# Loading the positions and the bias table from GpSimd's queue instead of SP's, in a two-layer encoder trunk

## The chip, the core and the metric

The kernel runs on one core of a Trainium2 chip. A core has engines that each work through their own queue of instructions: TensorE (PE) multiplies matrices, VectorE (DVE) and ScalarE (ACT) do elementwise work and reductions, GpSimd (POOL) does a little of that and issues DMAs, and SyncE (SP) issues most of the DMAs. ScalarE issues a few as well. Engines wait for each other and for DMAs through semaphores; within an engine's queue, an instruction that waits holds up everything behind it.

The metric is the device time of one execution in microseconds (us); the time of a kernel is the median of its runs.

## What is computed

A trunk of two layers over 256 tokens of width 2048, in float32. Each layer is an attention sub-layer (12 mixer heads and 4 heads into 256 memory tokens, one combined input projection, one output projection) and a squared-ReLU MLP of width 8192. All mixer heads of both layers add a relative-position bias, which is looked up in a small table by the distance of two positions:

```python
def t5_bucket(rel):
    half = N_BUCKETS // 2
    max_exact = half // 2
    side = jnp.where(rel > 0, half, 0)
    n = jnp.abs(rel)
    n_f = jnp.maximum(n, 1).astype(jnp.float32)
    large = max_exact + (jnp.log(n_f / max_exact) / math.log(MAX_DISTANCE / max_exact)
                         * (half - max_exact)).astype(jnp.int32)
    large = jnp.minimum(large, half - 1)
    return side + jnp.where(n < max_exact, n, large)

def rel_bias_lookup(rel_bias, rel):
    return jnp.take(rel_bias, t5_bucket(rel), axis=0)
...
for i in range(DEPTH):
    h = rms_norm(x, norm_attn[i])
    ...
    proj = h @ w_in_a[j]                  # layer 0; w_in_b in layer 1
    ...
    x = x + heads @ w_out[i]
    h = rms_norm(x, norm_mlp[i])
    x = x + jnp.square(jax.nn.relu(h @ w_up[i])) @ w_down[i]
```

The change touches the inputs of that lookup: the 256 integer positions, and `rel_bias`, the table of 32 buckets by 12 heads.

## The kernel before

**Tiling.** Every float32 product is made of three passes: an operand is split into `hi`, its value rounded to a shorter float, and `lo`, what is left; the passes are hi by hi, hi by lo and lo by hi. For a weight, ScalarE casts the loaded `raw` to `hi` (L355) and VectorE subtracts to get `lo` (L356). For the activations of the first chunk, ScalarE makes the `hi` half of `x` with the norm's gain (L351) and VectorE its `lo` half (L352).

**The first chunk.** Layer 0's input projection goes in chunks of 512 output columns (`chunk_tok`, L414). A chunk has 8 pieces of 512 KB, a piece has two blocks of 128 rows of k, and a block is 6 matmuls (L426 to L428): two groups of tokens by three passes. That makes 16 blocks and 96 matmuls a chunk. In the first chunk only (`lead=first`), each piece is loaded in two halves, one for each block, and before each block `first` loads parts of the input `xs` from ScalarE's queue (L994) and makes that block's `x`. From the second chunk on, whole pieces are fetched ahead (`fetch`, L303). `raw`, `hi` and `lo` have four buffers each, so SP's next weight load waits until VectorE has made the `lo` of the piece four before.

**Tasks.** Small work is cut into stages and put between pieces. `tick` (L163), called after each piece, runs the next stage of the first task that is due. `prep` (L1014) is the task that prepares the bias; it becomes due 5 ticks after the start. Its stages are:

- `bias_distance` (L705): two loads by SP, the positions along the free dimension on all 128 partitions (`pq`, a `t1k` buffer, L707) and the positions by partition (`pk`, an `sm` buffer, L709); two subtractions on GpSimd (L712); a cast to float on VectorE (L714).
- `bias_size` (L716) and three times `bias_steps` (L722): the bucket number by compares and adds on VectorE (L718, L719, L724).
- `bias_side` (L726): the sign's half on VectorE (L728, L730), and a store of the bucket numbers to DRAM as `bkt` (L731).
- `bias_table` (L733): `tab` is cleared on VectorE (L735), four copies of the table are loaded by SP (L737), and it is split in three parts of short floats (L741, L743).

After that, eight tasks (`bias_hot`, `bias_rows`) load `bkt` back from GpSimd's queue (L756) spread over the partitions, compare it with the bucket numbers on VectorE (L758), and use TensorE to look up the bias (L767).

**Order.** The text of the kernel gives priorities, not the final order in each engine's queue: when the program is built, an instruction may be set earlier than its place in the text if it is expected to be ready. The trace shows this: the clearing of `tab` (L735) and GpSimd's L747, both from the last stage of `prep`, run in the first 2 us. In the queue of one engine the built order is fixed.

Of the kernel before, what the change touches and what calls it, by code (L numbers as in the profile page):

```python
# [17 lines left out]
I32 = mybir.dt.int32  # L18
# [4 lines left out]
P = 128  # L23
S = 256
# [32 lines left out]
def trunk(ctx: ExitStack, tc: tile.TileContext, xin, xtok, memin, pos, rel, gcol, rows,  # L57
          w_a, w_b, w_mem, w_out, w_up, w_down, out):
    nc = tc.nc
# [10 lines left out]
    def nm(s):  # L70
        uid[0] += 1
        return f"{s}{uid[0]}"
# [25 lines left out]
    def big(shape):  # L98
        return xp.tile(shape, F32, tag="big", name=nm("big"), bufs=1)

    def t2k(shape, dt=F32):
        return tp.tile(shape, dt, tag="t2k", name=nm("t2k"), bufs=6)

    def t1k():
        return tp.tile([P, 256], F32, tag="t1k", name=nm("t1k"), bufs=4)

    def small(n):
        return tp.tile([P, n], F32, tag="sm", name=nm("sm"), bufs=36)
# [593 lines left out]
    bsv = dp.tile([P, 12 * 2 * S], F32, name="bsv")  # L702
    tabs = {}

    def bias_distance():  # L705
        pq = t1k().bitcast(I32)
        nc.sync.dma_start(pq, pos.rearrange("(a s) -> a s", a=1).broadcast_to([P, S]))  # L707
        pk = small(2).bitcast(I32)
        nc.sync.dma_start(pk, pos.rearrange("(t p) -> p t", p=P))  # L709
        dl = t2k([P, 2, S], I32)  # L710
        for t in range(2):
            nc.gpsimd.tensor_tensor(dl[:, t, :], pk[:, t:t + 1].broadcast_to([P, S]), pq, op=ALU.subtract)  # L712
        tabs["f"] = t2k([P, 2, S])
        nc.vector.tensor_copy(tabs["f"], dl)  # L714
# [7 lines left out]
    def bias_steps(*at):  # L722
        for thr in at:
            nc.vector.scalar_tensor_tensor(tabs["b"], tabs["n"], float(thr), tabs["b"], op0=ALU.is_ge, op1=ALU.add)  # L724
# [8 lines left out]
    def bias_table():  # L733
        tab = cp.tile([P, 48], F32, name="tab")
        nc.vector.memset(tab, 0.0)  # L735
        for g in range(4):
            nc.sync.dma_start(tab[32 * g:32 * g + 32, 12 * g:12 * g + 12], rel)  # L737
        parts = []
        for i in range(3):
            part = cp.tile([P, 48], BF16, name=f"tab{i}")  # L740
            nc.vector.tensor_copy(part, tab)  # L741
            if i < 2:
                nc.vector.tensor_tensor(tab, tab, part, op=ALU.subtract)  # L743
            parts.append(part)
        it = cp.tile([P, 1], I32, name="iti")
        for g in range(4):
            nc.gpsimd.iota(it[32 * g:32 * g + 32, :], pattern=[[0, 1]], base=0, channel_multiplier=1)  # L747
        itf = cp.tile([P, 1], F32, name="itf")
        nc.vector.tensor_copy(itf, it)
        tabs["parts"], tabs["iota"] = parts, itf  # L750
# [251 lines left out]
    def first(k):  # L1002
# [5 lines left out]
        elif k % 2 == 0:  # L1008
# [2 lines left out]

    bias = big([P, 12, 2, S])
    Task([scalars], wait=4)
    prep = Task([bias_distance, bias_size, lambda: bias_steps(12, 16), lambda: bias_steps(23, 32), lambda: bias_steps(46, 64, 91),  # L1014
                 bias_side, bias_table], wait=5, gap=1)
    rows_done = [Task([lambda i=i: bias_hot(i), lambda i=i: bias_rows(i, bias)], [prep], wait=BW) for i in range(8)]
# [112 lines left out]
```

## Time and profile before

| | us |
|---|---|
| median of 3 runs | 2106.43 |
| the runs | 2107.10, 2103.86, 2106.43 |
| the profiled execution | 2105.52 |
| its span, first to last instruction | 2103.7 |

The profile is taken from one execution. Its views name a line and an engine, the tile written and the tiles read (`out<-in`), the shape and the count; a bracket at the end of a row says how long the engine stood idle before it and what it waited for. `SPq`, `ACTq` and `POOLq` rows are DMA issues or waits of that engine's queue; the transfer itself goes on after the issue. Starts are in us from the first instruction. Matmul rows last longer than the step from one matmul to the next, because matmuls are pipelined.

Before the change, SP's queue has the first eight weight loads (0.75 to 7.78 us), then a load of parameter rows, one of the four table loads (8.38), and then weight loads with the positions, parts of the residual input (L1000) and the other three table loads in between, up to 24.55 us.

### The profile page before, as it was taken

To read this page: it belongs to the slowest core of one execution; us is meant where nothing else is said; L and a number is where in the kernel's file an instruction comes from. 1 tells how busy PE (TensorE), PEld (TensorE's weight loads), DVE (VectorE), ACT (ScalarE), POOL (GpSimd) and SP (SyncE) were. 2 spreads that over 40 slices of the span, in tenths; PEclk is the share of its full clock that TensorE was granted. 3 is DMA by queue.
4 is the path that set the end of the run, shared out by engine and by line. 5 is a ranking of instruction groups with operands and counts; after the bars stand their busy time and mean duration, and the time that the engine had idled before them with its cause. 6 is when DMAs were issued, how large, how long until landed. Compare 5 with 4: busy or idle time off the path is not lost.

```text
span 2103.7 us, 30034 instructions
## 1 busy us (share of the span) xinstructions
PE 2094.0 (100%) x10924; PEld 1773.7 (84%) x10924; DVE 1641.4 (78%) x2463; ACT 1175.7 (56%) x1782; POOL 115.8 (6%) x211
## 2 busy tenths in 40 slices
PE   9999999999999999999999999999999999999999
PEld 7878878888888888888888888888888888888887
DVE  7667788866666679999996678886676667999998
ACT  6466585554444456656655556554444445666664
POOL 1200020000011000000000000000001100000000
PEclk9999999999999999999999999999999999999999
DMA  8865554677788778878866656457788977888884
GB/s 293 239 209 154 164 183 159 186 236 238 255 298 304 257 244 277 299 242 274 304 241 205 180 164 184 159 178 250 256 267 300 310 230 279 272 285 288 287 292 145
DMA packets 150452, 504.18 MB, mean 240 GB/s; under 512 B 17952, under 2 KB 18720, under 8 KB 150048
## 3 DMA queue, kind: packets, MB, share of 16 engines
q1 hardware_dynamic: 129696, 433.53, 63.0%
q0 software_dynamic: 19168, 66.60, 9.9%
q10 hardware_dynamic: 1440, 2.15, 0.3%
q8 instruction: 85, 1.39, 0.3%
q14 instruction: 63, 0.52, 0.1%
HBM read 464.85 MB, written 37.36 MB: 239 GB/s over the span
## 4 chain that ended last, share of the span: by engine, by line
PE 97%; DMA 1%; DVE 1%; ACT 1%; issue 0%; SPq 0%; POOL 0%; POOLq 0%
PE mm L439 11%; PE aux L439 11%; PE mm L466 7%; PE mm L467 7%; PE aux L467 7%; PE aux L466 7%; PE mm L465 7%; PE aux L465 7%; PE mm L426 6%; PE mm L427 6%; PE mm L428 6%; PE mm L443 6%; PE aux L443 6%; DMA raw<-in_w_a 1%; PE aux L567 1%; PE aux L538 1%
## 5 line engine op out<-in xcount | busy, mean ns | idle before, releaser
L356 DVE TENSOR_TENSOR lo<-raw,hi 128x1024 fp32r<-128x1024 f32 (+1 forms) x616 | 739.7, 1212 | 364.6 <-ACT hi L355 361.4
L355 ACT CAST hi<-raw 128x1024 fp32r<-128x1024 f32 (+1 forms) x616 | 632.2, 1040 | 576.6 <-PE mm L439 158.9
L426 PE MATMUL mm<-hi,x 128*128 128x512 f32 x640 | 256.7, 403 | 0.6 <-ACT hi L355 0.6
L427 PE MATMUL mm<-lo,x 128*128 128x512 f32 x640 | 251.9, 394 | 2.2 <-DVE lo L356 2.0
L428 PE MATMUL mm<-hi,x 128*128 128x512 f32 x640 | 251.7, 393 | 0.0
L439 PE MATMUL mm<-x,hi 128*128 128x512 f32 x1024 | 246.9, 391 | 0.0
L439 PE MATMUL aux<-x,hi 128*128 128x512 f32 x1024 | 246.9, 391 | 0.0
L439 PEld LDWEIGHTS mm<-x,hi 128*128 128x128 f32 x1024 | 188.2, 188 | 36.4
L439 PEld LDWEIGHTS aux<-x,hi 128*128 128x128 f32 x1024 | 188.2, 188 | 36.4
L355 ACT CAST x<-big 128x1024 fp32r<-128x1024 f32 x106 | 110.6, 1053 | 142.0 <-DVE big L291 114.8
L465 PE MATMUL mm<-hi,h 128*128 128x512 f32 x446 | 174.0, 390 | 0.0
L466 PE MATMUL mm<-lo,h 128*128 128x512 f32 x446 | 173.6, 389 | 0.0
L467 PE MATMUL mm<-hi,h 128*128 128x512 f32 x446 | 173.5, 389 | 0.0
L465 PE MATMUL aux<-hi,h 128*128 128x512 f32 x444 | 172.9, 390 | 0.0
L467 PE MATMUL aux<-hi,h 128*128 128x512 f32 x444 | 172.6, 389 | 0.0
L466 PE MATMUL aux<-lo,h 128*128 128x512 f32 x444 | 172.6, 389 | 0.0
L427 PEld LDWEIGHTS mm<-lo,x 128*128 128x128 f32 x640 | 121.0, 189 | 25.4 <-DVE lo L356 3.8
L428 PEld LDWEIGHTS mm<-hi,x 128*128 128x128 f32 x640 | 120.6, 188 | 25.5
L426 PEld LDWEIGHTS mm<-hi,x 128*128 128x128 f32 x640 | 120.8, 189 | 24.6 <-ACT hi L355 1.0
L443 PEld LDWEIGHTS aux<-x,lo 128*128 128x128 f32 x1024 | 131.3, 191 | 5.0
L443 PEld LDWEIGHTS mm<-x,lo 128*128 128x128 f32 x1024 | 131.1, 191 | 4.8
L443 PE MATMUL mm<-x,lo 128*128 128x256 f32 x1024 | 133.0, 283 | 0.0
(269 smaller groups left out, 3120.2 us busy)
## 6 DMA issues: line engine op xcount, KB each, us to landing
raw<-in_w_up SPq DMA_DIRECT2D x256, 512.0 KB, 4.6
raw<-in_w_down SPq DMA_DIRECT2D x140, 512.0 KB, 4.6
big<-in_w_down SPq DMA_DIRECT2D x97, 512.0 KB, 5.0
raw<-in_w_a SPq DMA_DIRECT2D x72, 512.0 KB, 3.9
h<-kept POOLq DMA_DIRECT2D x58, 512.0 KB, 5.8
raw<-in_w_out SPq DMA_DIRECT2D x52, 512.0 KB, 3.7
raw<-in_w_b SPq DMA_DIRECT2D x48, 512.0 KB, 3.7
raw<-in_w_mem SPq DMA_DIRECT2D x32, 512.0 KB, 3.8
```

Source lines behind the costliest of these rows:

```text
L355: nc.scalar.copy(hi, src)
L356: return nc.vector.tensor_tensor(lo, src, as32(hi), op=ALU.subtract)
L426: nc.tensor.matmul(ps[t], lhsT=xh, rhs=hi[:, ws], start=(k == 0), stop=False)
L427: nc.tensor.matmul(ps[t], lhsT=xh, rhs=lo[:, ws], start=False, stop=False)
L428: nc.tensor.matmul(ps[t], lhsT=xl, rhs=hi[:, ws], start=False, stop=(k == KT - 1))
L439: nc.tensor.matmul(ps[o], lhsT=hi[:, cols(k % 2, o)], rhs=x2.rearrange("p a s -> p (a s)"), start=(k == 0), stop=(k == 2 * nj - 1))
L443: nc.tensor.matmul(ps[o][:, 256:512], lhsT=lo[:, cols(k % 2, o)], rhs=x2[:, 0, :], start=False, stop=False)
L465: nc.tensor.matmul(acc_, lhsT=x(0), rhs=w2[0][:, ws], start=first_, stop=False)
L466: nc.tensor.matmul(acc_, lhsT=x(0), rhs=w2[1][:, ws], start=False, stop=False)
L467: nc.tensor.matmul(acc_, lhsT=x(1), rhs=w2[0][:, ws], start=False, stop=last_)
L538: nc.tensor.transpose(out=pt[:, h * P:(h + 1) * P], in_=qn[t][:, h * P:(h + 1) * P], identity=ident)
L567: nc.tensor.transpose(out=pt[:, kt * S + qt * P:kt * S + (qt + 1) * P], in_=p_of(qt)[:, kt * P:(kt + 1) * P], identity=ident)
```

## The change

The two position loads leave `bias_distance` for a function of their own, `bias_positions`, which is called before the first chunk, right behind the creation of the first task and ahead of `prep`. They are issued by `nc.gpsimd` instead of `nc.sync`. The four loads of the table stay where they are in the text, and are issued by `nc.gpsimd` too. The buffers, sizes and shapes of the loads and everything computed from them stay as they were.

```diff
@@ -702,11 +702,15 @@
+    def bias_positions():
+        pq = t1k().bitcast(I32)
+        nc.gpsimd.dma_start(pq, pos.rearrange("(a s) -> a s", a=1).broadcast_to([P, S]))
+        pk = small(2).bitcast(I32)
+        nc.gpsimd.dma_start(pk, pos.rearrange("(t p) -> p t", p=P))
+        tabs["p"] = pq, pk
+
     def bias_distance():
-        pq = t1k().bitcast(I32)
-        nc.sync.dma_start(pq, pos.rearrange("(a s) -> a s", a=1).broadcast_to([P, S]))
-        pk = small(2).bitcast(I32)
-        nc.sync.dma_start(pk, pos.rearrange("(t p) -> p t", p=P))
+        pq, pk = tabs["p"]
         dl = t2k([P, 2, S], I32)
@@ -734,7 +738,7 @@
         tab = cp.tile([P, 48], F32, name="tab")
         nc.vector.memset(tab, 0.0)
         for g in range(4):
-            nc.sync.dma_start(tab[32 * g:32 * g + 32, 12 * g:12 * g + 12], rel)
+            nc.gpsimd.dma_start(tab[32 * g:32 * g + 32, 12 * g:12 * g + 12], rel)
@@ -1011,6 +1015,7 @@
     bias = big([P, 12, 2, S])
     Task([scalars], wait=4)
+    bias_positions()
     prep = Task([bias_distance, bias_size, lambda: bias_steps(12, 16), lambda: bias_steps(23, 32), lambda: bias_steps(46, 64, 91),
```

## The prediction

> **What bounds the kernel now.** I read the page first: the busy shares and the chain that ended last.
>
> ```profile
> span 2103.7 us, 30034 instructions
> PE 2094.0 (100%) x10924; PEld 1773.7 (84%) x10924; DVE 1641.4 (78%) x2463; ACT 1175.7 (56%) x1782; POOL 115.8 (6%) x211
> PE 97%; DMA 1%; DVE 1%; ACT 1%; issue 0%; SPq 0%; POOL 0%; POOLq 0%
> ```
>
> TensorE is busy for 2094.0 of 2103.7 us and makes up 97% of the chain. Nothing that the change touches runs on TensorE, so it can only win where TensorE waits or runs slowly. The next view is that of TensorE's waits over the whole run.
>
> ```profile
> PE mm L427 <- DVE lo L356: 2.0, 1, 2.0
> PE aux L567 <- DVE t2k L606: 1.3, 1, 1.3
> ...
> PE mm L426 <- ACT hi L355: 0.6, 1, 0.6
> ```
>
> One wait stands out: 2.0 us, once, at a matmul of the first kind of chunk, for the `lo` half of a weight. The timeline shows where it is and what stood in VectorE's queue there (VectorE, GpSimd and SP rows, then TensorE).
>
> ```profile
> 19.78 0.68 DVE L356 TENSOR_TENSOR lo<-raw,hi 128x512 fp32r<-128x512 f32 x1
> 22.93 0.43 DVE L714 CAST t2k<-t2k 128x512 f32<-128x512 int32 x1 [2.46 <-POOL t2k L712]
> 23.39 0.69 DVE L718 SCALAR_TENSOR_TENSOR t2k<-t2k 128x512 f32<-128x512 f32 x1
> 24.00 0.48 DVE L352 SCALAR_TENSOR_TENSOR x<-xs,gc,x 128x256 fp32r<-128x256 f32 x1
> 24.39 0.68 DVE L356 TENSOR_TENSOR lo<-raw,hi 128x512 fp32r<-128x512 f32 x1
> 25.00 0.48 DVE L352 SCALAR_TENSOR_TENSOR x<-xs,gc,x 128x256 fp32r<-128x256 f32 x1
> ...
> 21.71 1.18 POOL L712 TENSOR_TENSOR t2k<-sm,t1k 128x256 int32<-128x256 int32 x2 [19.84 <-DMA sm<-in_pos]
> 13.72 0.45 SPq L707 DMA_DIRECT2D t1k<-in_pos  x1
> 16.48 0.43 SPq L709 DMA_DIRECT2D sm<-in_pos  x1
> 21.73 2.82 SPq L737 DMA_DIRECT2D tab<-in_rel  x3
> ...
> 6.98 0.47 PE L426 MATMUL mm<-hi,x 128*128 128x512 f32 x1
> 22.50 0.61 PE L426 MATMUL mm<-hi,x 128*128 128x512 f32 x2
> 25.13 0.50 PE L427 MATMUL mm<-lo,x 128*128 128x512 f32 x1 [2.01 <-DVE lo L356]
> ```
>
> SP issues the second position load at 16.48; GpSimd's subtraction waits for it until 21.71. VectorE's cast L714 comes next in its queue, so VectorE stands still for 2.46 us, and the x and `lo` halves of block 10 come only at 24.00 and 24.39. TensorE runs dry at 23.11 and resumes at 25.13. A table by stage shows the aftermath; its columns are the stretch, then busy times, and at the end the granted clock, the DMA share and GB/s.
>
> ```profile
> 7.00:23.00 16.00, 15.30 (x64) 11.20 (x63) 10.46 (x24) 11.64 (x26) 1.18 (x2) 1.00 1.00 346
> 23.00:25.00 2.00, 0.12 (x1) 0.00 (x0) 1.97 (x5) 0.86 (x2) 0.00 (x0) 1.00 1.01 342
> 25.00:30.00 5.00, 4.87 (x14) 3.91 (x15) 5.00 (x12) 2.84 (x5) 0.00 (x0) 0.66 0.68 209
> 30.00:35.00 5.00, 5.00 (x23) 4.12 (x22) 3.52 (x6) 3.77 (x8) 0.00 (x0) 1.00 0.90 247
> ```
>
> After the wait the clock is 0.66 for about 5 us, with 14 matmuls where the next 5 us hold 23. So the late positions cost TensorE a wait and a spell of low clock. Everything to win lies in the first 35 us.
>
> **The change, part by part.** The chunk has 16 blocks of k, 6 matmuls each, 96 in all. First the pace, from two starts 36 matmuls apart, and how many matmuls were done when TensorE ran dry (groups of lines up to 23.2 us).
>
> ```profile
> 30.97 0.39 PE L428 MATMUL mm<-hi,x 128*128 128x512 f32 x1
> 39.13 0.39 PE L428 MATMUL mm<-hi,x 128*128 128x512 f32 x1
> ...
> L427 PE MATMUL mm<-lo,x 128*128 128x512 f32 x20 | 8.1, 407 | 0.1
> L428 PE MATMUL mm<-hi,x 128*128 128x512 f32 x20 | 7.8, 392 | 0.0
> L426 PE MATMUL mm<-hi,x 128*128 128x512 f32 x22 | 7.8, 400 | 0.6 <-ACT hi L355 0.6
> ```
>
> The pace is 8.16 / 36 = 0.227 us. By 23.11, 62 of the 96 are done. Before: 1 more at 25.13 and 14 in the slow stretch make 77 by 30.0; the other 19 take 4.3 us, so the chunk ends at about 34.35.
>
> *The wait removed.* With the positions there early, VectorE goes on with block 10 at 19.78 + 0.68 = 20.46. What ScalarE has ready then, and what is late next, its own rows tell:
>
> ```profile
> 19.98 0.60 ACT L355 CAST hi<-raw 128x512 fp32r<-128x512 f32 x1
> 22.85 0.50 ACT L351 ACTIVATE x<-xs,gc 128x256 fp32r<-128x256 f32 x1
> 26.06 0.51 ACT L351 ACTIVATE x<-xs,gc 128x256 fp32r<-128x256 f32 x1 [2.19 <-DMA xs<-in_xin]
> 27.30 0.62 ACT L355 CAST hi<-raw 128x512 fp32r<-128x512 f32 x1 [0.73 <-DMA raw<-in_w_a]
> 28.24 0.60 ACT L355 CAST hi<-raw 128x512 fp32r<-128x512 f32 x1
> ```
>
> The weight of block 10 is cast from 19.98 to 20.58, so nothing keeps VectorE from it. Block 13's x comes at 22.85, block 14's only at 26.06, its weight at 27.30. From 23.11 TensorE has 4 matmuls of block 10 left and 18 of blocks 11 to 13: 22 x 0.227 = 5.0 us, to 28.1. Block 14's `hi` is done at 27.92 and its `lo` 0.68 later at 28.6; the second matmul wants it at 28.3, so TensorE loses about 0.3. Block 15 (`hi` by 28.84, `lo` by 29.5) is in time. The end is 23.11 + 34 x 0.227 + 0.3 = 31.1, with no wait long enough to look like the one that went before the slow stretch. The gain is 34.35 - 31.1 = **3.25 us**, of which about 2.0 is the wait and the rest the clock, less the new 0.3. Even with no further wait the gain from here is 3.5.
>
> *SP's side.* The two position loads and four table loads leave SP's queue. Their issue time there costs TensorE nothing directly: none of its waits names SP. What it could be worth is that the last weight and x transfers start sooner; but the DMA share is already 1.00 at 346 GB/s from 7 to 23 us, so I count nothing, and keep 0 to 2 us (rival 2).
>
> *GpSimd's side.* Six DMAs are issued on GpSimd, which is idle from 1.9 us until 21.71. What they cost there and how long they take to land I bound by these rows, the last of which is GpSimd's own later DMAs:
>
> ```profile
> t1k<-in_pos SPq DMA_DIRECT2D x1, 128.0 KB, 6.2
> sm<-in_pos SPq DMA_DIRECT2D x1, 1.0 KB, 5.1
> blk<-bkt POOLq DMA_DIRECT2D x32, 128.0 KB, 8.6
> 49.14 4.02 POOL L756 DMA_DIRECT2D blk<-bkt  x8 [26.25 <-DMA bkt<-t1k]
> ```
>
> An issue is 4.02 / 8 = 0.50 us, so six take 3.0 us; only the two subtractions L712 are behind them before 49.14. Issued from about 2 us, the second position load lands between 3.0 + 5.1 = 8.1 and 3.0 + 8.6 = 11.6; L712 twice (1.2) makes it ready at 9.3 to 12.8, against 22.9 now. The 128 KB compete with the first weights and x: 0.131 MB / 346 GB/s = 0.38 us, between 0 (the same bytes leave the later, also full, stretch) and 0.8 (if the small ones cost as much again). I take **0.38**. [...]
>
> *VectorE's new order.* L714 and the steps behind it (L718 and on) may now come earlier between two blocks, where TensorE has no reserve. L714 and L718 take 24.00 - 22.93 = 1.07 us. VectorE's pitch is 25.00 - 24.00 = 1.0 us a block against TensorE's 6 x 0.227 = 1.36, so such a delay is made good in three blocks, later on free. The nearest row is another filler put between blocks 3 and 4:
>
> ```profile
> 13.00 0.29 DVE L788 TENSOR_TENSOR t1k<-rw 128x128 f32<-128x128 f32 x1 [0.59 <-DMA rw<-in_rows]
> 14.66 0.19 PEld L427 LDWEIGHTS mm<-lo,x 128*128 128x128 f32 x1 [0.57 <-DVE lo L356]
> 7.72 0.48 DVE L352 SCALAR_TENSOR_TENSOR x<-xs,gc,x 128x256 fp32r<-128x256 f32 x1 [1.40 <-ACT x L351]
> ```
>
> L788 and its partner held VectorE for some 1.1 us, wait included, and the weight load behind waited 0.57. The bounds are 0 and, with a long wait for the positions, the 5.5 us of rival 3; I take **0.57**.
>
> **Sum:** 3.25 - 0.38 - 0.57 = 2.3 us less. What comes after is paced by TensorE and moves up with it: the bias chain behind the positions moves up too, and the weights are fetched as buffers come free. The profiled execution took 2105.52 us, 1.8 around its span; less 2.3 that is 2103.2. The median of the three runs is 0.9 above that execution, so the forecast is **2104.1 us**.
>
> **The rivals.**
>
> 1. *The front stays bound by its bytes* (18%). The DMA share of 1.00 speaks for it: if the last x and weights land 2 or 3 us later because the small loads now push everything behind the first pieces, or if L714 now waits elsewhere, TensorE ends the chunk near 34 again. [...] Against it: 27.30 for the last weights but one is three us before TensorE wants more, and no byte is added. Here too belongs that the change does not do what it says, because GpSimd's loads come late in its queue; but GpSimd stands idle from 1.9 us. Gain 0 to 1: 2105.4 to 2106.4.
>
> 2. *More comes free* (12%). If the loads taken from SP's queue let the last x and weights start 2 us sooner and the first blocks lose nothing either, TensorE runs from 6.98 without any wait: 96 x 0.227 = 21.8, end 28.8, gain 5.5: 2100.9. Against it: DMA is full, and the first blocks wait for data (the 1.40 above) that the change can only delay.
>
> 3. *Slower: VectorE waits for the positions at the head of the chunk* (10%). L714 is set right behind block 0, ahead of the x that now starts at 7.72, and the load from GpSimd takes the 8.6 us of its later ones. Then L712 is done at 12.8, L714 at 13.2, and block 1 starts 5.5 us late. From there 90 matmuls take 20.4 us: first matmul at 13.7, and `lo` 0.5 after it, makes 34.6, plus 1.6 for another slow spell (14 matmuls where 5 us hold 21 or more): 36.2, and early small waits on top. That is 2 us slower, 2108.3; with 1 or 2 more from weight buffers freed late it passes 2110. It decides from a readiness of about 10.5 us on: up to there a place behind block 0 costs under 3 us. [...]
>
> **How the numbers follow.** The forecast (gain 1 to 3.5 us) has 60%, the rivals 18, 12 and 10. Runs of the same kernel lie 2103.86 to 2107.1, so a median may be 1 us off or more. The range goes from the forecast's best (2102.9) less 1.6 to rival 1's 2106.4 and a little beyond: 2101.3 to 2107.5. A difference of 0.2%, 4.2 us, is about what a measurement of this kernel can tell from none. Faster by that: most of rival 2 and a part of the forecast by scatter, 0.21. Slower by that: half of rival 3, 0.05. Within: 0.74.
>
> **What would show it.** Right: no wait of VectorE at L714 near 20 us; no TensorE wait of 2 us; the clock 1.00 from 25 to 30; the first chunk's last matmul near 31 to 32 and every later stage earlier by the same 2 to 3 us. The DMA cost is right if the first blocks start some 0.4 us later; the filler cost if L714 and L718 sit between early blocks. Wrong: VectorE waits at L714 before 13 us, the clock falls in another place, or x and weights of blocks 14 and 15 land after 30.

## The result, and the profile after

The changed kernel is slightly slower: median 2108.87 us (20 runs, 2103.69 to 2111.15) against 2105.47 us for the kernel before (20 runs, 2102.94 to 2109.38). The ratio is 1.0014, with a 95% interval of 1.0007 to 1.0020, so some 3 us are lost where 2.3 us were forecast to be won. The profiled execution took 2107.80 us. In the changed kernel the line numbers are higher: the positions load at L707 and L709, the subtractions are L716, the cast to float L718, `bias_size` starts at L722, the bias tiles load at L760, their compare is L762 and TensorE's lookups are L771.

First the head of the page, the shares of the chain that ended last, and TensorE's waits (us in total, times, longest).

```profile
span 2106.0 us, 30041 instructions
PE 2094.3 (99%) x10924; PEld 1774.2 (84%) x10924; DVE 1641.6 (78%) x2463; ACT 1175.5 (56%) x1782; POOL 118.5 (6%) x217
PE 95%; DMA 3%; DVE 1%; ACT 1%; issue 0%; POOL 0%; SPq 0%; ACTq 0%; POOLq 0%
```

```profile
PE aux L771 <- DVE blk L762: 2.9, 1, 2.9
PE mm L426 <- ACT hi L355: 1.9, 2, 1.6
```

The 2.0 us wait for a `lo` half is gone from the list. A new one heads it: 2.9 us, once, at the lookups of the bias, behind VectorE's compare. The next table is that of the kernel after by stage (stretch, busy times of PE, PEld, DVE, ACT, POOL, then clock, DMA share, GB/s); below it are two stretches of the kernel before.

```profile
7.00:23.00 16.00, 13.77 (x52) 10.09 (x51) 12.22 (x28) 10.52 (x23) 2.29 (x6) 0.89 0.99 349
23.00:25.00 2.00, 2.00 (x10) 1.67 (x9) 2.00 (x5) 0.98 (x3) 0.00 (x0) 1.00 1.09 340
25.00:30.00 5.00, 5.00 (x23) 4.14 (x23) 4.99 (x11) 4.12 (x9) 0.00 (x0) 1.00 0.92 315
...
70.00:75.00 5.00, 2.13 (x13) 1.44 (x12) 2.90 (x4) 1.42 (x2) 2.01 (x5) 1.00 1.01 257
75.00:80.00 5.00, 5.00 (x58) 4.24 (x59) 2.45 (x3) 1.52 (x2) 0.64 (x2) 0.66 1.05 262
```

```profile
70.00:75.00 5.00, 5.00 (x66) 4.36 (x65) 2.35 (x3) 2.39 (x3) 2.16 (x5) 1.00 1.03 284
75.00:80.00 5.00, 5.00 (x66) 4.17 (x65) 2.51 (x3) 1.73 (x3) 2.39 (x5) 1.00 1.04 271
```

From 23 to 30 us TensorE is now busy throughout at full clock, as forecast. But from 70 to 75 us it works only 2.13 of 5 us, and from 75 to 80 us the clock is 0.66, where the kernel before had 5.00 and 1.00 in both. There is a low clock in the front too: 0.89 from 7 to 23 us, behind a wait of 1.59 us at 7.86.

To see what each stage is worth, I count TensorE's matmuls in the trace and compare the start of the n-th one with that of the n-th in the profile before. Negative is earlier. The first chunk's 96 matmuls are the 33rd to the 128th; the 501st lies behind the lookups of the fourth bias tile.

| n-th matmul | start before, us | after: difference |
|---|---|---|
| 61st, in the first chunk | 15.23 | +1.90 |
| 128th, last of the first chunk | 34.37 | -2.06 |
| 261st | 62.12 | -2.06 |
| 501st | 80.70 | +2.59 |
| last | 2099.36 | +2.43 |

So the front did win 2.06 us, and 4.65 us were lost between the 261st and the 501st matmul: 2.87 of wait, and the slow stretch behind it, 0.34 x 5 = 1.7. After that nearly nothing changes.

**Where the 4.65 us went.** Here are the rows of the timeline around the fourth bias tile (start, duration, engine, line, operation; in brackets the idle time before and what ended it), first before, then after.

```profile
34.37 0.39 PE L428 MATMUL mm<-hi,x 128*128 128x512 f32 x1
...
70.09 1.05 ACT L355 CAST hi<-raw 128x1024 fp32r<-128x1024 f32 x1 [2.16 <-PE mm L428]
71.18 1.22 DVE L356 TENSOR_TENSOR lo<-raw,hi 128x1024 fp32r<-128x1024 f32 x1
72.31 0.75 DVE L758 TENSOR_SCALAR blk<-blk,itf 128x2048 bf16<-128x2048 bf16 x1
75.75 1.38 PE L767 MATMUL aux<-tab,blk 128*128 128x48 bf16 x48
```

```profile
32.31 0.39 PE L428 MATMUL mm<-hi,x 128*128 128x512 f32 x1
...
71.89 1.04 ACT L355 CAST hi<-raw 128x1024 fp32r<-128x1024 f32 x1 [2.23 <-DMA raw<-in_w_a]
72.97 1.22 DVE L356 TENSOR_TENSOR lo<-raw,hi 128x1024 fp32r<-128x1024 f32 x1 [1.96 <-ACT hi L355]
74.11 0.75 DVE L762 TENSOR_SCALAR blk<-blk,itf 128x2048 bf16<-128x2048 bf16 x1
74.91 1.44 PE L771 MATMUL aux<-tab,blk 128*128 128x48 bf16 x48 [2.87 <-DVE blk L762]
```

In both kernels VectorE's built order has the compare of this tile right behind the split of the last weight piece of a column chunk (it bears the number 3 and is the third to be worked on). Before, the compare was done at 73.06 and TensorE came for it at 75.75, a margin of 2.69 us. Three things eat it up. TensorE is 2.06 us earlier. The lookups stand 8 matmuls earlier in TensorE's built order: after 252 matmuls of the L426 to L428 stream instead of 260, worth 8 x 0.227 = 1.82. And the compare starts 1.80 later (74.11 for 72.31), because the cast ahead of the split waited for its weight to land, where before it had waited only for TensorE to free a buffer. 2.69 - 2.06 - 1.82 - 1.80 = -2.99, close to the 2.87 of the bracket. None of the three alone would have used up the margin.

The tile's own data were not what was missing. The last of its four loads is issued at 55.32 and had landed at 65.69, by the chain of work that leads to the lookups:

```profile
55.32 10.37 DMA blk<-bkt
```

They are early, not late: GpSimd begins to load the tiles at 43.99, where before it began at 49.14.

```profile
43.99 3.88 POOL L760 DMA_DIRECT2D blk<-bkt  x8 [32.51 <-DMA bkt<-t1k]
```

### The profile page after: what moved, and what is told of

Its sections match the earlier page's. It is cut to its first block, busy times and chain, and to the rows that moved or that the text cites. A ratio compares the mean times of both kernels' runs of the same rounds, so it can differ in the third digit from the quotient of the medians.

```text
span 2106.0 us, 30041 instructions
## 1 busy us (share of the span) xinstructions
PE 2094.3 (99%) x10924; PEld 1774.2 (84%) x10924; DVE 1641.6 (78%) x2463; ACT 1175.5 (56%) x1782; POOL 118.5 (6%) x217
## 4 chain that ended last, share of the span: by engine, by line
PE 95%; DMA 3%; DVE 1%; ACT 1%; issue 0%; POOL 0%; SPq 0%; ACTq 0%; POOLq 0%
PE mm L439 11%; PE aux L439 11%; PE mm L466 7%; PE aux L466 7%; PE mm L467 7%; PE mm L465 7%; PE aux L467 7%; PE aux L465 7%; PE mm L443 6%; PE aux L443 6%; PE mm L426 6%; PE mm L427 6%; PE mm L428 6%; DMA blk<-bkt 1%; PE aux L567 1%; DMA xs<-in_xin 1%
## 5 line engine op out<-in xcount | busy, mean ns | idle before, releaser
L426 PE MATMUL mm<-hi,x 128*128 128x512 f32 x640 | 257.9, 404 | 1.9 <-ACT hi L355 1.9
L428 PE MATMUL mm<-hi,x 128*128 128x512 f32 x640 | 251.8, 393 | 0.0
L426 PEld LDWEIGHTS mm<-hi,x 128*128 128x128 f32 x640 | 120.9, 189 | 26.6 <-ACT hi L355 3.1
L428 PEld LDWEIGHTS mm<-hi,x 128*128 128x128 f32 x640 | 120.9, 189 | 25.6
```

Source lines behind the costliest of these rows:

```text
L426: nc.tensor.matmul(ps[t], lhsT=xh, rhs=hi[:, ws], start=(k == 0), stop=False)
L428: nc.tensor.matmul(ps[t], lhsT=xl, rhs=hi[:, ws], start=False, stop=(k == KT - 1))
```

## Experiments

Four theories stood at the start. **A**: the front wins, and the win is given back at the fourth tile because in the built orders TensorE's lookups stand ahead of the place where VectorE has their compare ready. **B**: the weights of that chunk come too late with the DMA engines full (share 1.01 from 70 to 75 us), whatever the order. **C**: the table loads on GpSimd's queue are to blame. **D**: it is GpSimd's queue itself, carrying the positions. In each run "difference" is that of the 61st, 128th, 501st and last matmul against the profile before, as above. Kernels with added lines have shifted line numbers; the tile names tell what is meant.

**1 and 2: the fourth tile's lookups one step later, in both kernels.**

```diff
-    rows_done = [Task([lambda i=i: bias_hot(i), lambda i=i: bias_rows(i, bias)], [prep], wait=BW) for i in range(8)]
+    def look_up(i):
+        if i == 3:
+            Task([lambda: bias_rows(i, bias)], wait=1, gap=1, front=True)
+        else:
+            bias_rows(i, bias)
+    rows_done = [Task([lambda i=i: bias_hot(i), lambda i=i: look_up(i)], [prep], wait=BW) for i in range(8)]
```

> The changed kernel, with the lookups of the fourth bias tile put one tick later on TensorE (24 matmuls behind those of the third tile; 12 in the changed kernel, 20 in the one before). Theory A (the change wins about 2 us in the first chunk; it is given back because TensorE now meets the fourth tile's lookups before VectorE has compared that tile): the wait of 2.9 us and the low clock behind it go, no TensorE wait over 0.5 us between 60 and 80 us, span about 2 us below that of before (ratio 0.9985 to 0.9995). Theory B (the weights come too late in this stretch, because the bias tiles are now loaded 5 us sooner through a full DMA): TensorE waits for a weight half instead, 2 us or more, and the time stays at that of the changed kernel (ratio 1.0005 to 1.002).

> The kernel before with the same lookups one tick later: the partner of the run above, with the same order on TensorE. Theories A and B: as before within 1 us (ratio 0.9995 to 1.0005), since TensorE waited for nothing in this stretch. If it gains or loses 1 us or more by itself, the tick has a price of its own, which is to be taken off the run above.

In both kernels the lookups of tile 4 now come after 264 matmuls, and those of the later tiles 12 later as well. On the changed kernel: 2104.07 us, ratio 0.9998 (0.9989 to 1.0007); on the kernel before: 2105.65, ratio 1.0005 (0.9997 to 1.0014). Differences +1.31, -2.21, -1.44, +0.17 and -0.61, -1.53, -1.02, -0.21. The wait on the changed kernel:

```profile
75.21 1.38 PE L771 MATMUL aux<-tab,blk 128*128 128x48 bf16 x48 [0.41 <-DVE blk L762]
```

The wait fell from 2.87 to 0.41 and no low clock followed (1.00 from 75 to 80 us), so the place of the lookups matters as A says. The median of run 1 is 1.6 us below that of run 2, but not below that of the kernel before by the 0.05 to 0.15% that I had expected. From the 501st matmul to the last, run 1 falls back by 1.6 us. About half of that is no loss: with another order the n-th matmul is another one, and run 2, whose order is the same as that of run 1, falls back by 0.8 in this count too. Between the two runs, 0.8 us of the lead is lost by the end; the lists of TensorE's waits explain about 0.4 of it, two waits of 0.2 us, and the rest is open.

**3 and 4: one part of the change at a time.** Run 3 has the positions on GpSimd and the tables back on SP; run 4 has the positions early but issued by SP, and the tables on GpSimd.

```diff
-            nc.gpsimd.dma_start(tab[32 * g:32 * g + 32, 12 * g:12 * g + 12], rel)
+            nc.sync.dma_start(tab[32 * g:32 * g + 32, 12 * g:12 * g + 12], rel)
```

```diff
-        nc.gpsimd.dma_start(pq, pos.rearrange("(a s) -> a s", a=1).broadcast_to([P, S]))
+        nc.sync.dma_start(pq, pos.rearrange("(a s) -> a s", a=1).broadcast_to([P, S]))
...
-        nc.gpsimd.dma_start(pk, pos.rearrange("(t p) -> p t", p=P))
+        nc.sync.dma_start(pk, pos.rearrange("(t p) -> p t", p=P))
```

> The changed kernel with the four table loads back on SP's queue: only the positions are loaded by GpSimd. Theory A: the cost at the start and the lookups' wait come with the positions, so all stays as in the changed kernel: x of block 1 on VectorE near 8.9 us, the wait of about 2.9 us at the fourth tile, ratio 1.0005 to 1.002. Theory C (the four small table loads on GpSimd's queue hold up the first weights and x): x of block 1 returns to 7.7 to 8.2 us.

> The changed kernel with the two position loads at the same place in the text, but issued by SP ahead of the first weight (the tables stay with GpSimd). Theory A (the early place, and not the engine, gives the new order and the wait): the wait at the fourth tile stays, 2 to 4 us, ratio 1.000 to 1.002. Theory D (the loss comes from GpSimd's queue itself, which takes more DMA time for the same bytes): the first chunk starts some 0.5 us later for the two issues, but x of block 1 comes sooner than 8.9 us, no low clock before 23 us, and the time falls below that of before (ratio under 0.9995).

Run 3: 2110.26 us, ratio 1.0026 (1.0015 to 1.0036), differences +1.41, -2.30, +3.72, +3.28. Run 4: 2105.99, ratio 1.0011 (1.0002 to 1.0020), differences +1.66, -2.25, +3.23, +3.12. Their lookups of tile 4, one row from each:

```profile
76.39 2.10 PE L771 MATMUL aux<-tab,blk 128*128 128x48 bf16 x48 [2.87 <-DVE blk L762]
```

```profile
75.58 1.53 PE L771 MATMUL aux<-tab,blk 128*128 128x48 bf16 x48 [3.48 <-DVE blk L762]
```

Without the tables on GpSimd, and without the positions on GpSimd, the front wins the same 2.3 us and the same wait takes it back. So the win comes from the early place of the position loads, and not from the queue that issues them. Both have the lookups at 252 matmuls. C and D are out as the main cause. Run 3 has a second wait, 1.55 us at the lookups of tile 3, and is the slowest of these kernels.

**5: the compare ahead of the split.** TensorE's order is exactly that of the changed kernel; only VectorE makes the compare of tile 4 ahead of the split of the last piece of chunk 3.

```diff
-                done[0] = split(hi[:, s], lo[:, s], raw[:, s])
+                if (name, c, j) == ("a", 3, 7):
+                    nc.scalar.copy(hi[:, s], raw[:, s])
+                    with tc.issue_after(compared[3].ins):
+                        done[0] = nc.vector.tensor_tensor(lo[:, s], raw[:, s], as32(hi[:, s]), op=ALU.subtract)
+                else:
+                    done[0] = split(hi[:, s], lo[:, s], raw[:, s])
...
-        nc.vector.tensor_scalar(hot, hot, tabs["iota"][:, 0:1], None, op0=ALU.is_equal)
+        compared[i] = nc.vector.tensor_scalar(hot, hot, tabs["iota"][:, 0:1], None, op0=ALU.is_equal)
```

> The changed kernel; VectorE makes the compare of the fourth bias tile ahead of the lo half of the last piece of column chunk 3 instead of behind it. TensorE's order stays exactly as in the changed kernel (lookups of that tile after 252 matmuls). Theory A (the gain was given back because TensorE's lookups stand ahead of where VectorE's order has their compare ready): the compare runs near 71 us instead of 74.1, the 2.9 us wait at the lookups falls below 0.5, no low clock in 70-80, median 2103.5-2105.3, ratio 0.9990-1.0003. Theory B (the weights of chunk 3 come too late, whatever the order): TensorE then waits 1.5 us or more for hi or lo of a weight between 70 and 85 us instead, and the ratio is 1.0008 or more.

2102.48 us, ratio 0.9990 (0.9981 to 0.9999), differences +1.08, -2.46, -2.46, -2.80. This is the decisive run: with one 0.75 us instruction in another place the profiled span falls from 2106.0 to 2100.8. Of these 5.2 us, 4.65 are the stretch from the 261st to the 501st matmul, where this run loses nothing. Its timeline:

```profile
70.72 1.05 ACT L338 CAST hi<-raw 128x1024 fp32r<-128x1024 f32 x1 [2.06 <-DVE blk L768]
74.00 1.06 ACT L361 CAST hi<-raw 128x1024 fp32r<-128x1024 f32 x1 [1.84 <-DMA raw<-in_w_a]
...
69.93 0.74 DVE L768 TENSOR_SCALAR blk<-blk,itf 128x2048 bf16<-128x2048 bf16 x1
71.81 1.23 DVE L340 TENSOR_TENSOR lo<-raw,hi 128x1024 fp32r<-128x1024 f32 x1 [1.14 <-ACT hi L338]
...
71.48 1.38 PE L777 MATMUL aux<-tab,blk 128*128 128x48 bf16 x48
```

The compare runs at 69.93 without waiting for anything, so its data were there; the lookups at 71.48 have no bracket, and the split comes after. And TensorE's waits have no new entry at a weight:

```profile
PE mm L432 <- ACT hi L361: 1.2, 2, 0.7
PE aux L124 <- DVE tab L745: 1.1, 1, 1.1
PE aux L573 <- DVE t2k L612: 1.0, 1, 1.0
```

B asked for 1.5 us or more at a weight between 70 and 85 us, and is refuted as a bound on TensorE. What B had right is that casts still wait for weights to land there (the 1.84 of the row at 74.00). That is what made the split, and through the order the compare, late; with the compare out from behind it, the weights come just in time.

**6: the early loads held back.** As run 5, and the 128 KB position load waits until the x parts of block 3 are there: it is issued at 10.67 us, with the table loads around it (10.13 to 12.70). The 1 KB position load still goes out at 1.30.

```diff
+        nc.gpsimd.tensor_copy(pq[:, 0:1], xs[0][:, 3, 0:1].bitcast(I32))
         nc.gpsimd.dma_start(pq, pos.rearrange("(a s) -> a s", a=1).broadcast_to([P, S]))
...
+        if k == 2:
+            bias_positions()
```

> As the kernel before in this list, and the position loads on GpSimd's queue are held until the x parts of block 3 have landed (near 9 us), so that they no longer share the DMA engines with the first weights and x. If the early loads cost the first blocks about 2 us: the 60th matmul comes 1.3 to 2 us sooner than in the changed kernel (lag to the kernel before within 0.6 instead of +1.9), the first chunk ends 1 us sooner still, and the median is 0.5-1.5 us below the run before in this list, ratio 0.9985-0.9998. Rival: the bytes that the first blocks lose come back before the chunk's end anyway, so the chunk ends at the same time within 0.5 us and the medians agree within 0.5 us. VectorE's cast of the distances (near 17 us in the changed kernel) may wait up to 1 us.

2105.08 us, ratio 1.0004 (0.9995 to 1.0013), differences -0.07, -0.85, -0.85, -1.00. The 61st matmul comes 1.15 sooner than in run 5, which has the same other edit, so the early loads do cost the first blocks that much. (Against the changed kernel it is 1.97, but that profile has a spell of low clock in its front.) But VectorE's cast now waits, and x and `lo` of the next blocks with it:

```profile
18.03 0.43 DVE L725 CAST t2k<-t2k 128x512 f32<-128x512 int32 x1 [2.50 <-POOL t2k L723]
...
19.10 0.48 DVE L358 SCALAR_TENSOR_TENSOR x<-xs,gc,x 128x256 fp32r<-128x256 f32 x1
```

TensorE waited 2.6 us behind it; I had expected at most 1 us at the cast, and missed.

**7: control.** The edit of run 5 on the kernel before.

> Control: the kernel before the change with only the shift of the compare on VectorE. TensorE did not wait at these lookups there, so theory A expects no difference: ratio 0.9994-1.0006. If it is faster by 1 us or more, the compare's place is worth something by itself and theory A's reading of the run with the changed kernel is weakened.

2104.99 us, ratio 1.0001 (0.9993 to 1.0010), differences -0.43, -1.76, -1.76, -1.54. The compare's place is worth nothing that can be measured where TensorE comes later than the compare. The differences show something else: with an unchanged front, this profile is 1.76 us ahead of the profile before at the 128th matmul, though it has a wait of 2.2 us at the same place. Its clock did not fall behind the wait:

```profile
23.00:25.00 2.00, 0.00 (x0) 0.00 (x1) 1.97 (x5) 0.94 (x3) 0.00 (x0) 1.00 0.84 267
25.00:30.00 5.00, 5.00 (x22) 4.15 (x23) 4.93 (x10) 2.16 (x4) 0.00 (x0) 1.00 0.83 242
```

**8: the bias tiles' loads held back** in the changed kernel, until the first weight of chunk 3 is cast.

```diff
+        if (name, c, j) == ("a", 3, 0):
+            tabs["gate"] = hi
...
+        if i == 0:
+            nc.gpsimd.tensor_copy(hot[:, 0:1], as32(tabs["gate"][:, 0:1]))
         for g in range(4):
```

> The changed kernel; the eight bias tiles' loads on GpSimd are held until the first weight of chunk 3 is cast (48.2 us; they began at 43.99 in the changed kernel and 49.14 before). The builder then sets the lookups later too (after 216, 228, 244, 266 matmuls instead of 216, 228, 240, 252). Theory A: the wait at tile 4's lookups is gone because of their place, and the last weight of chunk 3 still lands near 71-72 us; median 2103.5-2105.3. Theory B: it lands near 70 us as in the kernel before, because the tiles' bytes come later. If a wait of over 1 us stays at the lookups in spite of the later place, the lateness of the tiles' own data is a third cause.

2104.32 us, ratio 0.9999 (0.9991 to 1.0008), differences +0.87, -2.67, -1.63, -2.30. The largest wait at any lookup is 0.8 us, at an earlier tile. The cast of the last weight of chunk 3:

```profile
68.40 1.05 ACT L357 CAST hi<-raw 128x1024 fp32r<-128x1024 f32 x1 [2.35 <-PE mm L430]
```

It is at 68.40 instead of 71.89, and it waits for TensorE again, not for the weight: with the bias tiles' bytes later, the weight is in time, which is B's part of the chain. The lookups moved as well: 244 and 266 matmuls for tiles 3 and 4 here, 240 and 252 in the changed kernel and in runs 3 to 6. In these kernels the lookups stand later where the bias chain is ready later; that the builder's estimate of this time sets their place fits, but no record of that estimate shows it. As both moved, this run alone doesn't tell which of them removed the wait.

**9: the held loads, with the cast of the distances behind block 11.**

```diff
+        with tc.issue_after(done[0].ins):
             nc.vector.tensor_copy(tabs["f"], dl)
```

> As the run with the held position loads, and VectorE's cast of the distances is set behind the lo half of block 11 instead of behind block 6, where it waited 2.50 us for GpSimd's subtractions. The bias tiles' lookups come after 216, 228, 246, 267 matmuls. If the early loads' cost at the first blocks and that wait were all that the front lost: lag at the 60th matmul within 0.6 us of the kernel before, no wait of over 1 us before 30 us, first chunk's end 2.5 to 3.5 us sooner than in the profile before, median 2101.5-2103.0, ratio 0.9980-0.9993. Rival: the chunk's end is set by its last x and weights all the same, and comes no sooner than in the run with only the shifted compare (2.46 us): median 2102.3-2103.5.

A miss: 2107.84 us, ratio 1.0015 (1.0006 to 1.0024), differences -0.53, -0.23, -0.14, +2.46. The wait at the cast only moved, and a late one came back:

```profile
17.64 0.19 DVE L753 CAST tab<-tab 128x48 bf16<-128x48 f32 x1 [2.56 <-DMA tab<-in_rel]
...
90.65 1.23 DVE L362 TENSOR_TENSOR lo<-raw,hi 128x1024 fp32r<-128x1024 f32 x1 [1.57 <-ACT hi L361]
91.79 0.75 DVE L770 TENSOR_SCALAR blk<-blk,itf 128x2048 bf16<-128x2048 bf16 x1
...
92.60 1.38 PE L779 MATMUL aux<-tab,blk 128*128 128x48 bf16 x48 [2.16 <-DVE blk L770]
```

Now it is the table's split on VectorE that waits, for the table loads that are held with the positions on GpSimd's queue. And at 92.60 the pattern of tile 4 appears at a later tile: a compare behind the split of a weight that came late. It is the same mechanism in a place I had not touched.

**10: the tables alone on GpSimd.** The edit is the one line of the kernel before; the positions stay on SP.

```diff
-            nc.sync.dma_start(tab[32 * g:32 * g + 32, 12 * g:12 * g + 12], rel)
+            nc.gpsimd.dma_start(tab[32 * g:32 * g + 32, 12 * g:12 * g + 12], rel)
```

> The kernel before with the four table loads alone on GpSimd's queue; the positions stay on SP's. Lookups after 216, 228, 245, 266 matmuls. My reading (the early positions carry the gain, the tables carry nothing): VectorE still waits for the positions near 20 us and TensorE 1 to 2.5 us behind it, no wait at the lookups; ratio 0.9990-1.0007. Rival (freeing SP's queue brings the last x and weights sooner): the first chunk ends 2 us sooner than in the profile before in spite of the wait, ratio below 0.9990.

2107.57 us, ratio 1.0012 (1.0003 to 1.0020), differences -0.15, +2.73, +4.07, +4.81. No gain from freeing SP's queue; the positions came later still, and I had not expected that:

```profile
26.23 0.43 DVE L714 CAST t2k<-t2k 128x512 f32<-128x512 int32 x1 [5.44 <-POOL t2k L712]
...
17.52 0.38 SPq L709 DMA_DIRECT2D sm<-in_pos  x1
...
27.31 0.80 PE L427 MATMUL mm<-lo,x 128*128 128x512 f32 x1 [4.33 <-DVE lo L356]
```

The second position load is issued 1.04 us later than before (17.52 for 16.48) and VectorE's wait is 5.44 instead of 2.46. So the positions, not the tables, are what the first chunk depends on. The profiled execution is the slowest of the 11 (2110.08), so the size of its wait is not typical.

**11: the edit of run 5 on run 4** (positions early but from SP).

> The positions early but issued by SP (that kernel alone was 2105.99, ratio 1.0011, with a wait of 3.48 us at the lookups), and now the fourth tile's compare ahead of the last split of column chunk 3. Theory A: the wait at the lookups falls below 0.5 us, the median by 3 to 5 us against that run, to 2101.5-2103.5, ratio 0.9982-0.9995. Theory B: the wait moves to a weight and the ratio stays above 1.0005.

2104.72 us, ratio 1.0001 (0.9992 to 1.0009), differences +2.07, -1.72, -0.61, -0.75. The 3.48 us wait is gone and no weight takes its place; a wait of 0.8 us is left at the lookups of tile 3, and the median fell by 1.3 us instead of 3 to 5. In its front VectorE waited 2.16 us for the parameter rows, which SP issues behind the positions:

```profile
14.78 0.29 DVE L798 TENSOR_TENSOR t1k<-rw 128x128 f32<-128x128 f32 x1 [2.16 <-DMA rw<-in_rows]
...
16.72 0.50 PE L433 MATMUL mm<-lo,x 128*128 128x512 f32 x1 [2.01 <-DVE lo L362]
```

**12: run 5 once more.**

> The changed kernel with the fourth tile's compare ahead of the last split of column chunk 3, once more, because its interval against the kernel before (0.9981 to 0.9999) nearly touches 1. If its gain is real: median 2101.5-2103.5, ratio 0.9983-0.9997, no wait over 0.5 us at the lookups of tile 4. If the first result was scatter: median 2104 or more, ratio 0.9997-1.0005.

2102.81 us, ratio 0.9991 (0.9982 to 1.0000), differences +0.97, -2.57, -2.57, -2.56. The interval of this run just touches 1, but the two runs agree, and each has its median below all other kernels here: the change does bring some 2 us, once the compare is taken out from behind the split.

## Why the prediction was wrong, step by step

- **The wait removed: right.** VectorE no longer waits at the cast (no bracket at its row, below), the clock is 1.00 from 23 to 30 us, and the chunk's last matmul starts at 32.31, 2.06 us earlier than before. I had said 31 to 32 and a net 2.3. That this is so close is partly luck. From the 61st matmul to the 128th the kernel before takes 34.37 - 15.23 = 19.14 us, the changed one 32.31 - 17.13 = 15.18, its bare pace (67 x 0.227 = 15.2): the gain there is 3.96, not 3.25. Block 14, for which I took off 0.3, caused no wait, and I had counted one matmul twice (the one at 25.13 is among the 14), which put the end before at 34.35 instead of 34.6. This error and that in the cost of the early loads, below, have opposite signs. And the clock fell elsewhere, which I had named as a sign of being wrong: it is 0.50 from 11.22 to 14.63 and from 76.07 to 79.48.

```profile
9.04 1.85 POOL L716 TENSOR_TENSOR t2k<-sm,t1k 128x256 int32<-128x256 int32 x2 [4.01 <-DMA sm<-in_pos]
...
8.92 0.48 DVE L352 SCALAR_TENSOR_TENSOR x<-xs,gc,x 128x256 fp32r<-128x256 f32 x1 [2.52 <-ACT x L351]
16.93 0.42 DVE L718 CAST t2k<-t2k 128x512 f32<-128x512 int32 x1
...
9.45 0.73 PE L426 MATMUL mm<-hi,x 128*128 128x512 f32 x2 [1.59 <-ACT hi L355]
```

- **Part of the 3.25 us was chance.** Runs 2 and 7 have the front of before, with waits of 1.5 and 2.2 us but no slow stretch behind them, and their 128th matmul is 1.53 and 1.76 us ahead of that profile. The 1.25 us that I counted for the clock belongs to some executions of the kernel before, not to all, so against its median less was to be won. The mean clock of each execution tells how many: of 105 executions of the kernel before that were timed beside the experiments, 29 have 0.999 and 76 have 1.000; one slow stretch, which costs 1.7 us of 2104, makes 0.9992. (A low clock behind the last matmul, 0.50 from 2101.74 us on in the profile before, enters this mean too, so the counts are an estimate.) The median of the 29 is 1.5 us above that of the 76. Of the 20 executions of the changed kernel 8 have 0.998, 8 have 0.999 and 4 have 1.000; of the 22 of runs 5 and 12, 18 have 1.000.
- **The early loads: mis-sized.** I took 0.38 for the bytes and 0.57 for fillers, 0.95 together. Measured at the 61st matmul it is 1.90, 1.31, 1.08 and 0.97 in the changed kernel and runs 1, 5 and 12; the 1.90 holds the low clock from 11.22 to 14.63, which the other three don't have. It comes with the loads: the x of block 1 on VectorE starts at 8.92 instead of 7.72, and held loads (run 6) bring the 61st matmul back to -0.07. It is the 128 KB of positions: with the positions alone early (run 3) the 61st matmul is at +1.41, with the tables alone (run 10) at -0.15. A cost of the fillers does not show: L718 and L722 stand behind block 5, and TensorE has no wait behind them.
- **GpSimd's side: right.** The subtractions end at 9.04 + 1.85 = 10.9, inside my 9.3 to 12.8, and rival 3's wait at the head of the chunk did not come.
- **The step that failed:** "What comes after is paced by TensorE and moves up with it: the bias chain behind the positions moves up too". TensorE did move up by 2.06 us. The bias chain moved up further: the loads of its tiles began 5.15 us earlier (43.99 for 49.14) and share the DMA engines (1.03 to 1.06 of their time from 50 to 70 us) with the weights of chunk 3; in run 8, where these loads are held, the last weight of chunk 3 is in time. So the compare of tile 4, which stands behind the split of such a weight, came 1.80 us later than before, and the lookups themselves stood 8 matmuls earlier. I treated the built order as given behind the front, though my own text said that an instruction is set by when it is expected to be ready: positions that are ready sooner reorder what hangs on them. I also never worked out the margin of each later meeting of TensorE with VectorE. It was in the trace of before: compare done at 73.06, lookups at 75.75, 2.69 us, and a gain of 2.3 us plus any change of order uses that up.
- **The rivals.** Rival 1 and rival 2 are not what happened: the chunk did end 2 us sooner. Rival 3 had the right kind of mechanism (an engine's fixed order puts something late ahead of what TensorE wants) in the wrong place; it was realised by my own edits in runs 6 and 9. The win comes from the earlier place and not from the other queue: run 10, where only the tables moved, shows no gain (ratio 1.0012), and run 4, where SP issues the early positions, wins as much in the front as GpSimd does (2.25 us against 2.06). The loss lies in an order and not in a transfer: in run 5, with the same loads and one compare in another place, the 4.65 us are not lost. The range ended at 2107.5, below the 2108.87 measured, because no rival let a later stage take back more than the front gave.

What stays open: about 0.4 us that run 1 loses against run 2 behind the 501st matmul, and why run 11 gained 1.3 us instead of 3 to 5.

## What to carry to other kernels

Before counting a gain at one place as a gain at the end, list the next meetings of the fast engine with the others and the margin at each; a gain larger than the smallest margin is given back there, and a spell of low clock behind the new wait can make it a loss (here 2.87 us of wait and 1.7 us of low clock against the 2.06 us won). When an input becomes ready sooner, ask what a built order will set earlier because of it, and what will then stand in front of what. A short instruction that TensorE waits for should not stand behind one that waits for a DMA: here that was a compare of 0.75 us, and with it in another place the profiled span fell by 5.2 us (run 5).

## What the runs showed of the hardware

The clock falls behind some short waits of TensorE and not behind others of the same size. It was low after waits of 2.01 (before), 1.59 and 2.87 (after), 2.87 (run 3), 3.48 (run 4), 2.29 (run 9) and 4.33 us (run 10), and stayed 1.00 after 1.5 (run 2), 2.2 (run 7), 2.6 (run 6) and 2.0 us (run 11). The traces show what tells them apart. Each slow stretch lasts 3.41 us at a clock of 0.50, so it costs a busy TensorE 1.7 us; run 10 has two in a row.

```profile
26.44:29.85 3.41, 3.41 (x10) 2.67 (x9) 3.41 (x8) 2.31 (x5) 0.00 (x0) 0.50 0.69 201
```

In one execution the clock changes only at whole multiples of 3.41 us from one another (11.22, 14.63, 76.07 and 79.48 in the changed kernel: 1, 18 and 1 of them). So I cut each profile into these periods and summed TensorE's idle time in each, up to its last matmuls. The eight periods ahead of a slow one hold 1.89 to 2.50 us of idle time (2.01 before, 1.89 and 2.25 after); all others hold 1.63 or less, but for one of 1.91 in run 11, behind which the clock stayed 1.00. The 2.2 us of run 7 straddle an edge, 0.95 and 1.25, and the clock stayed; the 2.01 us before the change lie in one period, and it fell. In these profiles, then, it is the idle time within one period that tells the slow stretches from the rest, but for the 1.91 of run 11; where the edges lie differs from execution to execution (26.44 and 29.85 before, 11.22 and 14.63 after, 4.46 periods from the one to the other). This is a reading of these profiles: no run here varied a wait alone to test it.

The position load issued beside the first weights delayed the x of block 1 by 1.2 us, three times the 0.38 that I had priced for its bytes at 346 GB/s. From 3 to 9 us the DMA engines are full in both kernels, 1.01 of their time before and 0.96 after, but they moved 356 GB/s before and 285 after:

```profile
3.00:9.00 6.00, 6.00 (x34) 5.40 (x33) 2.76 (x9) 2.15 (x4) 0.00 (x0) 1.00 1.01 356
```

```profile
3.00:9.00 6.00, 4.86 (x31) 4.25 (x30) 1.60 (x7) 1.74 (x4) 2.03 (x5) 1.00 0.96 285
...
q0 software_dynamic: 151, 0.14, 14.6%
```

The last row is the queue of GpSimd's loads from 0 to 9 us in the kernel after: packets, MB, and the share of the 16 engines' time that its packets took. 14.6% of 9 us are 1.3 us for 0.14 MB, about the delay that was seen. In run 10, with the tables alone, the share is 0.9%. So this load takes the engines' time far above its bytes.
